# Attention groups A and B of a two-layer encoder: one unit per step, or two units with dense products between

## Chip, cores and metric

The kernel runs on one core of a Trainium2 chip. The metric is the device time of one execution in microseconds (us). Its engines are named as in the profile: PE multiplies matrices (PEld is its loading of weights), DVE, ACT and POOL work element by element, SP issues most transfers (DMAs).

## What is computed

Two layers of an encoder on 1024 tokens of width 1024, all in float32. In each layer one projection feeds three groups of heads: A is attention over three dilations, B is windowed attention with a sink, C is a matrix memory (mLSTM) in both directions. Their outputs are joined, projected and added; a gated feed-forward network and a gated embedding follow.

```python
for i in range(DEPTH):
    h = rmsnorm(x, attn_norm[i])
    z = h @ w_in[i]
    ...
    ya = dilated_attention(qa, ka, va, bias_a)
    yb, _ = banded_attention(qb, kb, vb, bias_b, WINDOW_B, WINDOW_B, 1, sink=sink_logits[i])
    yc = mlstm_mixer(qc, kc, vc, oc, gc, qk_conv[i], gate_bias[i], mlstm_norm[i])
    x = x + concatenate([ya, yb, yc]) @ w_out[i]
    ...
```

## The kernel before

Activations lie with features on the 128 partitions and tokens along the free axis. A **dense** product (`product`, L210 to L223) computes 128 features by 512 tokens: for each of 8 slices of the input three matmuls of 128x512 (L219 to L221: high by high, high by low, low by high part), 24 in all, into one of two PSUM banks kept for it (tag "d"). The high and low parts of a weight tile come from `split` (L130 to L134): a cast on ACT (L133, tile `wh`) and a subtraction (L134, `wl`).

`mixers` runs three generators side by side (L1137): `attend` (group A in `group_a`, then group C in `group_c`), `project` (all dense products of the input projection, and the convolution of C) and `side` (C's gates, and `combine_a`, which joins A's dilations). `mix` (L60 to L84) goes on with the stream whose sum of yielded costs is lowest; a yield is thus a place where other streams' instructions may come in between, and its number says how much of the others. A second `mix` (L1224) runs group B beside the output projection.

**Group A** has 24 units per layer: 3 pairs of heads, 2 sets of dilations, 4 pairs of token tiles. For each unit `score` multiplies queries by keys (L531, L533, L539, tile `psc`, operands of 64 rows), adds bias and takes the maximum on DVE (L551), and the exponential on ACT (L552) into two tiles `pr`. `flip` transposes the two `pr` on PE (L565, `ppt`, 8 transposes) and copies them to two tiles `pT` (DVE L570, ACT L568). `weigh` multiplies values by `pT` (L586, `po`, 64 columns wide) and copies the result to `u` (DVE L589 to L594). In a step i the kernel issues score(i), weigh(i-2), flip(i-1), and then yields.

**Group B** has 16 units: 8 token tiles T by 2; `score` (L709), `flip` (L731), and per T one `weigh` (L754) and one `turn` (transposes of the scale, L764). It yields after each unit.

**combine_a** makes per pair of heads a small table (`mj`, `pst`, `join`), spreads it to four tiles `f` (ACT, L659), transposes each (PE L664, `pf`) and multiplies `u` by it (DVE L666).

**Group C** follows: values of the keys by exponents (`pk`, `ke`, `pl`, a scan along the pieces in `sc`, `cst`), then 8 pieces, of each `decay` (a DMA into two tiles `ee`, an edge cut on POOL, 12 exponentials on ACT), `score` (`pss`, `psi`, L992, L997) and `weigh` (`pso`, L1010 to L1023). `ee` and `it` come from a pool of 7 buffers (`aslot`), three for each piece.

The tiles `pr`, `pT`, `f`, `th` and many others come from one pool of half tiles, and there are ten:

```python
def half(self, s, dt=F32):
    return self.sm.tile([P, 512], dt, tag="s2", name=self.nm(s), bufs=10)
```

In layer 0 the input is not normalised ahead of the projection: each dense result is multiplied by `self.r[hf]`, two half tiles (`rs`, from `rstd`) that live until the last dense product of the projection has been copied out (L401). In layer 1 `self.r` is None.

The program's order is not the order of the Python calls alone. A scheduler takes the recorded instructions and their pools, and sets for each engine one fixed list; an instruction whose buffer isn't free is put behind others that can go. Each engine then runs its list in order.

Of the kernel before, what the change touches and what calls it, by code (L numbers as in the profile page):

```python
# [34 lines left out]
NCH = S // P  # L35
# [47 lines left out]
class Trunk:  # L83
# [388 lines left out]
    def group_a(self, z):  # L472
# [4 lines left out]
        units = [(p, g, i) for p in range(3) for g in range(2) for i in range(NCH // 2)]  # L477
# [3 lines left out]
        def tables(p):  # L481
            n = 2 * NCH * P
            va = self.att.tile([P, n + 768], F32, tag="va", name=self.nm("va"), bufs=2)
            b0, b1 = self.aslot("b").rearrange("p (h w) -> p h w", h=2), va[:, n:]
            eng = nc.sync if p else nc.gpsimd

            nc.gpsimd.memset(b0[0:64, :, 256:384], NEG)
            nc.gpsimd.memset(b0[64:128, :, 384:512], NEG)
            self.toeplitz(b0[:, :, 0:256], 0, 2 * p, 2, 256, 191, P, eng)
            self.toeplitz(b0[0:64, :, 384:512], 0, 2 * p, 2, P, 191, 64, eng)  # L490
            self.toeplitz(b0[64:128, :, 256:384], 0, 2 * p, 2, P, 255, 64, eng)
            for i in range(3):
                self.toeplitz(b1.rearrange("p (h i w) -> p h i w", h=2, i=3)[:, :, i], 1, 2 * p, 2, P, i * PL1 + 127, P, eng)
            st["b", p], st["va", p] = (b0, b1), va

        def begin(p):
            if p == 0:
                tables(p)
            n, va = NCH * P, st.pop(("va", p))
            vs = [va[:, i * n : i * n + n].rearrange("p (t h d) -> p t h d", t=NCH, h=2) for i in range(2)]  # L500
            vt = z.pop(("v", p))
            self.values([vt[:, T * P : T * P + P] for T in range(NCH)], vs[0])
            self.values([vt[:, T::8] for T in range(NCH)], vs[1])
            del vt
            st["v", p] = vs

            z["s", p] = self.sm.tile([P, 2, 2, 2, NCH], F32, tag="stat", name=self.nm("stat"), bufs=2)
            z["o", p] = self.aslot("u"), self.aslot("u")

        def tiles(g, i):  # L510
            return (2 * i, 2 * i + 1) if g == 0 else (i, i + 4)
# [9 lines left out]
        def score(u):  # L521
            p, g, i = u
            (qn, qr), kr = z["q", p], z["k", p]
            pss = [self.bank("psc") for _ in range(2)]
            for s, T in enumerate(tiles(g, i)):
                ws, ts = slice(s * 256, s * 256 + 256), slice(T * P, T * P + P)
                for e, hp in enumerate(heads):
                    k = kr[hp].rearrange("p (r n) -> p r n", r=8)
                    o = pss[e][:, ws]
                    if g == 1:  # L530
                        nc.tensor.matmul(o, qr[hp, ts], k[:, T % 4 :: 4], start=True, stop=True)  # L531
                    elif T < NCH - 1:
                        nc.tensor.matmul(o, qn[hp, ts], k[:, :, 16 * T : 16 * T + 32], start=True, stop=True)  # L533
                if g == 0 and T == NCH - 1:
                    for m, n in ((0, 112), (16, 0)):
                        for e, hp in enumerate(heads):
                            k = kr[hp].rearrange("p (r n) -> p r n", r=8)
                            o = pss[e][:, ws].rearrange("p (r m) -> p r m", r=8)[:, :, m : m + 16]
                            nc.tensor.matmul(o, qn[hp, ts], k[:, :, n : n + 16], start=True, stop=True)  # L539
            prs = [self.half("pr") for _ in range(2)]  # L540
            for s, T in enumerate(tiles(g, i)):
                w = slice(s * 256, s * 256 + 256)
                for e in range(2):
                    nm, zs = (z["s", p][:, g, j, e, T : T + 1] for j in range(2))
                    o, sc, b = prs[e][:, w], pss[e][:, w], bias(p, g, T, e)
                    if g == 0:
                        sc = sc.rearrange("p (r m) -> p m r", r=8)
                        o, b = (x.rearrange("p (m r) -> p m r", r=8) for x in (o, b))
                    else:
                        o, sc = (x.rearrange("p (i w) -> p i w", i=2) for x in (o, sc))  # L550
                    nc.vector.tensor_tensor_reduce(o, sc, b, -1.0, 3e38, OP.add, OP.min, nm)  # L551
                    nc.scalar.activation(prs[e][:, w], prs[e][:, w], AF.Exp, bias=nm, scale=-1.0, accum_out=zs)  # L552
            st[u] = prs
            if g == 1 and i == 3:
                z.pop(("q", p)), z.pop(("k", p)), st.pop(("b", p))

        def flip(u):
            p, g, i = u
            pTs = []
            for e, pr in enumerate(st[u]):  # L560
                pt = self.bank("ppt")
                for b in range(4):

                    c = b if g == 0 else b % 2 * 2 + b // 2
                    nc.tensor.transpose(pt[:, c * P : c * P + P], pr[:, b * P : b * P + P], self.ident)  # L565
                pT = self.half("pT")
                if e:
                    nc.scalar.copy(pT, pt)  # L568
                else:
                    nc.vector.tensor_copy(pT, pt)  # L570
                pTs.append(pT)
            st[u] = pTs

        def weigh(u):
            p, g, i = u
            pTs = st.pop(u)
            v = st["v", p][g]
            po = self.bank("po")[:, 0:256]
            T = 2 * i
            if g == 0:  # L580
                steps = ((T + 1, 128, 384, 0), (T, 0, 128, 0), ((T + 2) % NCH, 384, 512, 128))
            else:
                steps = ((i, 0, 256, 0), (i + 4, 256, 512, 0))
            for n, (t, c0, c1, o0) in enumerate(steps):
                for e, hp in enumerate(heads):
                    nc.tensor.matmul(po[hp, o0 : o0 + c1 - c0], v[:, t, e, :], pTs[e][:, c0:c1], start=n == 0, stop=n == len(steps) - 1)  # L586
            us = z["o", p][g]
            if g:
                nc.vector.tensor_copy(us.rearrange("p (r n) -> p r n", r=8)[:, i::4], po.rearrange("p (i n) -> p i n", i=2))  # L589
            elif i < 3:  # L590
                nc.vector.tensor_copy(us[:, 64 + T * P : 320 + T * P], po)
            else:
                nc.vector.tensor_copy(us[:, 832:1024], po[:, 0:192])
                nc.vector.tensor_copy(us[:, 0:64], po[:, 192:256])  # L594
            if g == 1 and i == 3:
                st.pop(("v", p))
                z["u", p] = True

        n = len(units)
        for i in range(n + 2):  # L600
            cost = 0.0
            if i < n:
                p = units[i][0]
                if units[i][1:] == (0, 0):
                    while ("k", p) not in z:
                        yield None
                    begin(p)
                    cost += 2000.0
                score(units[i])
                cost += 1000.0  # L610
                if units[i][1:] == (0, 3) and p < 2:
                    tables(p + 1)
            if 0 <= i - 2:
                weigh(units[i - 2])
                cost += 1000.0
            if 0 <= i - 1 < n:
                flip(units[i - 1])
                cost += 1000.0
            yield cost

    def combine_a(self, z):

# [51 lines left out]
    def group_b(self, li, z, yT):  # L674

        nc = self.nc
        units = [(T, j) for T in range(NCH) for j in range(2)]
        heads = (slice(0, 64), slice(64, 128))
        st = {}

# [91 lines left out]
        while "qb1" not in z:  # L772
            yield None
        begin()
        n = len(units)
        for i in range(n + 5):
            cost = 0.0
            if i < n:
                score(units[i])
                cost += 900.0  # L780
            if i % 2 == 1 and 0 <= i - 3 < n:
                weigh((i - 3) // 2)
                cost += 1600.0
            if i % 2 == 0 and 0 <= i - 4 < n:
                turn((i - 4) // 2)
                cost += 300.0
            if 0 <= i - 1 < n:
                flip(units[i - 1])
                cost += 700.0
            if cost:  # L790
                yield cost

    def turn(self, li, yT):

# [912 lines left out]
```

## Time and profile before

| | us |
|---|---|
| median of three runs (lowest, highest) | 2758.97 (2756.2, 2760.41) |
| the profiled execution, its span | 2764.66, 2762.9 |
| PE busy over the span | 2653.5 |
| DVE, ACT, POOL busy | 1874.0, 1129.6, 690.2 |

How to read it: the profiled execution is 5.7 us longer than the median, and 1.8 us lie around its span. The chain of work that ended last lies on PE for 82% of the span. Layer 0's groups A and C with the input projection stand from 61.7 to 465 us of the span, layer 1's from 1500 to 1817 us; group B stands from 485 to 564 us and from 1837 to 1915 us. Rows of the trace name an instruction by engine, line and tiles (out<-in); `x8` means eight instructions in a row; a product of float32 operands shows as two.

### The profile page before, as it was taken

The page shows a single profiled execution, that of the slowest core. Times are in us where ns is not written, and L with a number is a line of the kernel's source. Part 1 is how long each engine was busy: PE and PEld are TensorE (multiplying, and loading weights), DVE is VectorE, ACT ScalarE, POOL GpSimd, SP SyncE. Part 2 cuts the span into 40 slices and gives each one's busy share as a digit, 9 for nine tenths or more (in the row PEclk, how much of TensorE's full clock was granted, in tenths as well). Part 3 has the DMA queues.
Part 4 walks back from the last instruction along what each step waited for, and adds up shares of the span by engine and source line. Part 5 has one row for each costly group of instructions (what it writes and reads, how often), then busy time and mean ns, then how long its engine had stood idle before and what let it go on. Part 6 is the DMA issues. An engine that isn't in the chain of part 4 may idle for free.

```text
span 2762.9 us, 37720 instructions
## 1 busy us (share of the span) xinstructions
PE 2653.5 (96%) x13906; PEld 2118.3 (77%) x13906; DVE 1874.0 (68%) x3119; ACT 1129.6 (41%) x2317; POOL 690.2 (25%) x544
## 2 busy tenths in 40 slices
PE   7999988998999999999999999989899999999997
PEld 5777766676888888888777778867678888888887
DVE  8645776569877775755655448664897777685646
ACT  5443243544333334234444433544443333242444
POOL 3112434136333330000121122431553333100002
PEclk9999998998999999999999999989999999999998
DMA  4010145131333338752321012442233333496424
GB/s 148 28 66 24 46 107 155 72 137 58 145 145 126 141 111 311 268 168 92 123 77 54 31 39 67 116 154 74 106 114 132 139 136 122 162 330 226 156 69 137
DMA packets 165340, 339.34 MB, mean 123 GB/s; under 512 B 18233, under 2 KB 57185, under 8 KB 165156
## 3 DMA queue, kind: packets, MB, share of 16 engines
q1 hardware_dynamic: 161460, 325.27, 34.7%
q0 software_dynamic: 3696, 11.66, 1.2%
q8 instruction: 110, 1.80, 0.3%
q14 instruction: 74, 0.61, 0.1%
HBM read 246.56 MB, written 90.30 MB: 122 GB/s over the span
## 4 chain that ended last, share of the span: by engine, by line
PE 82%; DVE 8%; issue 3%; DMA 2%; POOL 2%; ACT 2%; SPq 0%; DVEq 0%; POOLq 0%; ACTq 0%
PE pd L1270 9%; PE pd L1271 9%; PE pd L1269 9%; PE pd L219 9%; PE pd L220 9%; PE pd L221 9%; PE pd L1438 5%; PE pd L1437 5%; PE pd L1436 5%; PE po L586 1%; PE ppt L565 1%; DVE x L1234 1%; PE psc L709 1%; PE po L754 1%; PE psc L533 1%
## 5 line engine op out<-in xcount | busy, mean ns | idle before, releaser
L1270 PE MATMUL pd<-r,wf 128*128 128x512 f32 x1232 | 491.0, 399 | 24.0 <-POOL r L1229 13.2
L1269 PE MATMUL pd<-r,wf 128*128 128x512 f32 x1232 | 488.4, 397 | 10.0 <-ACT r L1228 10.0
L1271 PE MATMUL pd<-r,wf 128*128 128x512 f32 x1232 | 486.4, 395 | 0.0
L219 PE MATMUL pd<-h,wh 128*128 128x512 f32 x832 | 340.1, 409 | 13.0 <-ACT h L133 7.1
L220 PE MATMUL pd<-h,wh 128*128 128x512 f32 x832 | 329.9, 396 | 3.2 <-DVE h L134 1.7
L221 PE MATMUL pd<-h,wl 128*128 128x512 f32 x832 | 328.2, 395 | 1.0 <-DVE wl L134 1.0
L1270 PEld LDWEIGHTS pd<-r,wf 128*128 128x128 f32 x1232 | 233.8, 190 | 85.5 <-POOL r L1229 19.9
L1269 PEld LDWEIGHTS pd<-r,wf 128*128 128x128 f32 x1232 | 233.6, 190 | 66.0 <-ACT r L1228 12.6
L1271 PEld LDWEIGHTS pd<-r,wf 128*128 128x128 f32 x1232 | 234.3, 190 | 52.5
L1437 PE MATMUL pd<-f,f 128*128 128x512 f32 x616 | 239.9, 389 | 1.1 <-DVE f L134 1.1
L1438 PE MATMUL pd<-f,f 128*128 128x512 f32 x616 | 239.7, 389 | 0.0
L1436 PE MATMUL pd<-f,f 128*128 128x512 f32 x616 | 236.3, 389 | 0.1
L1288 DVE TENSOR_TENSOR g<-g,pd 128x512 f32<-128x512 f32 x264 | 175.7, 680 | 60.7 <-PE pd L1271 59.1
L134 DVE TENSOR_TENSOR wf<-s,wf 128x512 fp32r<-128x512 f32 x176 | 161.9, 921 | 64.1 <-ACT wf L133 63.0
L133 ACT CAST wf<-s 128x512 fp32r<-128x512 f32 x176 | 106.5, 617 | 222.3 <-POOL s L200 63.9
L219 PEld LDWEIGHTS pd<-h,wh 128*128 128x128 f32 x832 | 158.2, 190 | 48.5 <-ACT h L133 7.1
L347 POOL TENSOR_TENSOR acc<-acc,sq 128x512 f32<-128x512 f32 (+1 forms) x22 | 29.6, 1344 | 654.5 <-ACT sq L346 654.2
L220 PEld LDWEIGHTS pd<-h,wh 128*128 128x128 f32 x832 | 158.5, 190 | 35.5 <-DVE h L134 2.6
L221 PEld LDWEIGHTS pd<-h,wl 128*128 128x128 f32 x832 | 158.2, 190 | 35.7 <-DVE wl L134 1.9
L134 POOL TENSOR_TENSOR wl<-wr,wh 128x1024 fp32r<-128x1024 f32 (+1 forms) x44 | 109.3, 2483 | 251.2 <-ACT wh L133 142.1
L134 DVE TENSOR_TENSOR f<-wr,f 128x512 fp32r<-128x512 f32 x132 | 90.1, 688 | 90.4 <-ACT f L133 86.3
L133 ACT CAST wh<-wr 128x1024 fp32r<-128x1024 f32 (+1 forms) x112 | 113.7, 1016 | 70.8 <-PE pd L220 49.4
(310 smaller groups left out, 5279.6 us busy)
## 6 DMA issues: line engine op xcount, KB each, us to landing
wr<-w_up SPq DMA_DIRECT2D x88, 512.0 KB, 4.3
bs<-wf SPq DMA_DIRECT2D x88, 512.0 KB, 2.7
f<-bs SPq DMA_DIRECT2D x176, 256.0 KB, 3.5
wr<-w_in SPq DMA_DIRECT2D x52, 512.0 KB, 3.6
wr<-w_down SPq DMA_DIRECT2D x88, 256.0 KB, 5.3
wr<-ple_gate SPq DMA_DIRECT2D x40, 512.0 KB, 3.5
bd<-g SPq DMA_DIRECT2D x66, 256.0 KB, 2.0
b<-bd SPq DMA_DIRECT2D x66, 256.0 KB, 5.6
```

The costliest lines, as they stand in the source:

```text
L133: self.pin(nc.scalar.copy(hi[:, cs], src))
L134: self.pin((eng or nc.vector).tensor_tensor(lo[:, cs], src, hi.bitcast(F32)[:, cs], OP.subtract))
L219: nc.tensor.matmul(ps, hi[:, ks], rh, start=k == 0, stop=False)
L220: nc.tensor.matmul(ps, hi[:, ks], rl, start=False, stop=False)
L221: nc.tensor.matmul(ps, lo[:, ks], rh, start=False, stop=k == n - 1)
L1269: nc.tensor.matmul(ps, hi[:, ks], rh, start=k == 0, stop=False)
L1270: nc.tensor.matmul(ps, hi[:, ks], rl, start=False, stop=False)
L1271: nc.tensor.matmul(ps, lo[:, ks], rh, start=False, stop=k == KT // 2 - 1)
L1288: add = lambda out, a, b, op=OP.add: nc.vector.tensor_tensor(out, a, b, op)
L1436: nc.tensor.matmul(ps, lh[:, cs], rh, start=k == 0, stop=False)
L1437: nc.tensor.matmul(ps, lh[:, cs], rl, start=False, stop=False)
L1438: nc.tensor.matmul(ps, ll[:, cs], rh, start=False, stop=k == NPAIR - 1)
```

## The change

Group A now takes units by twos. A step issues both scores, yields (so dense products of `project` come in), then issues the weighing of the preceding two units and the transposes of these two, and yields again. The yields sum to what they were. Group B does the same with the two units of a token tile; `turn` comes after the transposes, and the first step now yields 3300 with no `weigh` in it.

```diff
--- before.py
+++ after.py
@@ -596,27 +596,30 @@
                 st.pop(("v", p))
                 z["u", p] = True
 
-        n = len(units)
-        for i in range(n + 2):
-            cost = 0.0
-            if i < n:
-                p = units[i][0]
-                if units[i][1:] == (0, 0):
-                    while ("k", p) not in z:
-                        yield None
-                    begin(p)
-                    cost += 2000.0
-                score(units[i])
-                cost += 1000.0
-                if units[i][1:] == (0, 3) and p < 2:
-                    tables(p + 1)
-            if 0 <= i - 2:
-                weigh(units[i - 2])
-                cost += 1000.0
-            if 0 <= i - 1 < n:
-                flip(units[i - 1])
-                cost += 1000.0
-            yield cost
+
+        pairs = list(zip(units[::2], units[1::2]))
+        last = ()
+        for pair in pairs:
+            p = pair[0][0]
+            if pair[0][1:] == (0, 0):
+                while ("k", p) not in z:
+                    yield None
+                begin(p)
+                yield 2000.0
+            for u in pair:
+                score(u)
+            if pair[1][1:] == (0, 3) and p < 2:
+                tables(p + 1)
+            yield 2000.0
+            for u in last:
+                weigh(u)
+            for u in pair:
+                flip(u)
+            last = pair
+            yield 4000.0
+        for u in last:
+            weigh(u)
+        yield 2000.0
 
     def combine_a(self, z):
 
@@ -674,7 +677,6 @@
     def group_b(self, li, z, yT):
 
         nc = self.nc
-        units = [(T, j) for T in range(NCH) for j in range(2)]
         heads = (slice(0, 64), slice(64, 128))
         st = {}
 
@@ -772,23 +774,19 @@
         while "qb1" not in z:
             yield None
         begin()
-        n = len(units)
-        for i in range(n + 5):
-            cost = 0.0
-            if i < n:
-                score(units[i])
-                cost += 900.0
-            if i % 2 == 1 and 0 <= i - 3 < n:
-                weigh((i - 3) // 2)
-                cost += 1600.0
-            if i % 2 == 0 and 0 <= i - 4 < n:
-                turn((i - 4) // 2)
-                cost += 300.0
-            if 0 <= i - 1 < n:
-                flip(units[i - 1])
-                cost += 700.0
-            if cost:
-                yield cost
+        for T in range(NCH + 1):
+            if T < NCH:
+                for j in range(2):
+                    score((T, j))
+                yield 1800.0
+            if T:
+                weigh(T - 1)
+            if T < NCH:
+                for j in range(2):
+                    flip((T, j))
+            if T:
+                turn(T - 1)
+            yield 3300.0
 
     def turn(self, li, yT):
```

What the scheduler makes of it is shown at three places; lines in the changed file are two or three lower than before behind the edits.

**PE, group A of layer 1** (`psc` scores, `po` weighing, `ppt` transposes, `pd` dense). Before, one unit:

```order
L221 MATMUL pd_13612<-h_11814,wl_13258 128x512
L531 MATMUL psc_13664<-z_13130,z_12892 128x256
L531 MATMUL psc_13665<-z_13130,z_12892 128x256
L531 MATMUL psc_13664<-z_13130,z_12892 128x256
L531 MATMUL psc_13665<-z_13130,z_12892 128x256
L586 MATMUL po_13680<-pT_13643,va_12844 64x256
L586 MATMUL po_13680<-pT_13650,va_12844 64x256
L586 MATMUL po_13680<-pT_13643,va_12844 64x256
L586 MATMUL po_13680<-pT_13650,va_12844 64x256
L565 MATMUL ppt_13686<-ident,pr_13622 128x128 x4
L565 MATMUL ppt_13693<-ident,pr_13623 128x128 x4
L219 MATMUL pd_13612<-h_11820,wh_13257 128x512
```

Now, from the end of a pair's scores to the weighing of the preceding pair:

```order
L531 MATMUL psc_13647<-z_13144,z_12906 128x256
L219 MATMUL pd_13626<-h_11796,wh_13235 128x512
L220 MATMUL pd_13626<-h_11797,wh_13235 128x512
L221 MATMUL pd_13626<-h_11796,wl_13236 128x512
L219 MATMUL pd_13626<-h_11802,wh_13235 128x512
L220 MATMUL pd_13626<-h_11803,wh_13235 128x512
L221 MATMUL pd_13626<-h_11802,wl_13236 128x512
L586 MATMUL po_13668<-pT_13578,va_12814 64x256
L586 MATMUL po_13668<-pT_13585,va_12814 64x256
L586 MATMUL po_13668<-pT_13578,va_12814 64x256
L586 MATMUL po_13668<-pT_13585,va_12814 64x256
L586 MATMUL po_13674<-pT_13592,va_12814 64x256
```

Scores, weighing and transposes stood next to each other; now a run of dense products stands between scores and weighing, and each run is twice as long.

**ACT, layer 0, the joining of A's second pair of heads** (`f` the third of its four tiles, `wh` weight casts of the projection). Before:

```order
L552 ACTIVATE pr_2078,stat_1789<-pr_2078,stat_1789 128x256 x2
L568 COPY pT_2107<-ppt_2102 128x512
L659 COPY f_2113<-join_1925 128x512
L552 ACTIVATE pr_2136,stat_1789<-pr_2136,stat_1789 128x256 x2
L552 ACTIVATE pr_2137,stat_1789<-pr_2137,stat_1789 128x256 x2
L568 COPY pT_2167<-ppt_2162 128x512
L659 COPY f_2169<-join_1925 128x512
L133 CAST wh_2322<-wr_2055 128x1024
```

Now:

```order
L1110 ACTIVATE sg_3214<-sg_3214 128x512 x2
L133 CAST wh_3621<-wr_3413 128x1024
L133 CAST wh_3766<-wr_3619 128x1024
L133 CAST wh_3936<-wr_3764 128x768
L662 COPY f_2118<-join_1936 128x512
L568 COPY pT_2161<-ppt_2156 128x512
L568 COPY pT_2175<-ppt_2170 128x512
L662 COPY f_2180<-join_1936 128x512
L552 ACTIVATE pr_2212,stat_1803<-pr_2212,stat_1803 128x256 x2
```

The third `f` stood right behind its pair's exponentials, ahead of most weight casts. It now stands behind the projection's last weight cast (`wh_3936`), with A's last copies and exponentials behind it.

**PE, layer 0, from the end of group A to group C** (`pst`, `pf` the joining, `pvt` transposes of values, `pk`, `pl` group C). Before, in A's joining:

```order
L220 MATMUL pd_2387<-h_230,wh_2057 128x512
L221 MATMUL pd_2387<-h_229,wl_2058 128x512
L664 MATMUL pf_2396<-ident,f_2391 128x128 x4
L219 MATMUL pd_2387<-h_235,wh_2057 128x512
L220 MATMUL pd_2387<-h_236,wh_2057 128x512
L221 MATMUL pd_2387<-h_235,wl_2058 128x512
L219 MATMUL pd_2387<-h_241,wh_2057 128x512
L220 MATMUL pd_2387<-h_242,wh_2057 128x512
L221 MATMUL pd_2387<-h_241,wl_2058 128x512
L219 MATMUL pd_2387<-h_247,wh_2057 128x512
```

Now:

```order
L586 MATMUL po_2307<-pT_2282,va_1389 64x256
L640 MATMUL pst_2315<-mj_2313,div_111 64x32 x16
L447 MATMUL pvt_2332<-ident,z_2074 128x128 x4
L447 MATMUL pvt_2338<-ident,z_2074 128x128 x4
L667 MATMUL pf_2385<-ident,f_2380 128x128 x4
L667 MATMUL pf_2407<-ident,f_2399 128x128 x4
L667 MATMUL pf_2425<-ident,f_2417 128x128 x4
L667 MATMUL pf_2440<-ident,f_2434 128x128 x4
L447 MATMUL pvt_2446<-ident,z_2344 128x128 x4
L447 MATMUL pvt_2452<-ident,z_2344 128x128 x4
L921 MATMUL pk_2915<-ident,cv_2521 128x128 x4
L921 MATMUL pk_2924<-ident,cv_2521 128x128 x4
L935 MATMUL pl_2945<-vc_1806,ke_2920 64x65 x8
```

Before, dense products stood between all of these, and in group C too (15 to 21 between its runs). Now 717 dense matmuls stand in one run behind the scores of A's pair (third pair of heads, first set, tiles 4 to 7); the next row is the transposes of the late `f`, and from there to group C's last product no dense matmul is left. In layer 1 they still alternate.

## Rows read from the trace of the kernel before

**Rows 1.** Timeline of PE, 78.0 to 82.2 us: start, length, instructions.
```profile
78.26 0.39 PE L221 MATMUL pd<-h,wl 128*128 128x512 f32 x1
78.58 1.13 PE L531 MATMUL psc<-z,z 64*128 64x256 f32 x8
79.64 1.09 PE L586 MATMUL po<-pT,va 128*64 128x256 f32 x12
80.66 1.09 PE L565 MATMUL ppt<-ident,pr 128*128 128x128 f32 x8
81.51 0.48 PE L219 MATMUL pd<-h,wh 128*128 128x512 f32 x1
81.83 0.39 PE L220 MATMUL pd<-h,wh 128*128 128x512 f32 x1
82.06 0.40 PE L221 MATMUL pd<-h,wl 128*128 128x512 f32 x1
```

**Rows 2.** Timeline from 61.7 us: two units' scores in one run, the first exponential.
```profile
61.72 2.00 PE L533 MATMUL psc<-z,z 64*128 64x256 f32 x16
...
63.35 0.51 ACT L552 ACTIVATE pr<-pr,stat 128x256 f32<-128x256 f32 x1 [0.32 <-DVE stat L551]
```

**Rows 3.** PE's waits, 60 to 330 us: total us, times, longest.
```profile
PE pd L219 <- DVE z L401: 2.9, 1, 2.9
```

**Rows 4.** PE's waits, 330 to 365 us.
```profile
PE pl L937 <- DVE ke L926: 10.0, 2, 9.7
```

**Rows 5.** Three stretches: us, busy of PE, PEld, DVE, ACT, POOL, granted clock.
```profile
330.00:365.00 35.00, 24.85 (x182) 18.98 (x180) 29.49 (x27) 9.65 (x16) 11.18 (x7) 0.85 0.31 83
381.49:458.88 77.39, 77.39 (x737) 62.58 (x736) 48.69 (x113) 36.81 (x107) 31.01 (x33) 1.00 0.39 104
468.00:472.00 4.00, 0.00 (x0) 0.00 (x0) 1.30 (x5) 2.38 (x4) 1.41 (x2) 0.50 0.53 167
```

**Rows 6.** Groups of PE by line, 381.5 to 458.9 us: count, busy, mean ns.
```profile
L219 PE MATMUL pd<-h,wh 128*128 128x512 f32 x77 | 31.7, 411 | 0.0
```

**Rows 7.** Timeline of the joining of group A, 207 to 217 us.
```profile
208.06 0.41 DVE L631 TENSOR_TENSOR mj<-stat,mod 128x256 f32<-128x256 f32 x1
...
213.50 0.19 DVE L652 TENSOR_TENSOR join<-join 128x32 f32<-128x32 f32 x1
```

**Rows 8.** Groups by line, 60 to 480 us: count, busy us, mean ns.
```profile
L552 ACT ACTIVATE pr<-pr,stat 128x256 f32<-128x256 f32 x96 | 47.6, 497 | 48.2 <-DVE stat L551 48.2
...
L926 DVE TENSOR_TENSOR ke<-pk,cols 128x512 f32<-128x512 f32 x12 | 7.6, 680 | 1.4 <-PE pk L923 1.4
...
L946 DVE TENSOR_TENSOR_SCAN sc<-sc,sc 128x455 f32<-128x455 f32 x6 | 7.8, 1312 | 6.0 <-ACT sc L944 6.0
...
L832 DVE SCALAR_TENSOR_TENSOR cv<-th,cv 128x512 f32<-128x512 f32 x12 | 7.8, 688 | 3.6 <-ACT th L831 3.6
...
L937 PE MATMUL pl<-vc,ke 128*64 128x65 f32 x168 | 7.7, 242 | 10.0 <-DVE ke L926 10.0
```

**Rows 9.** Timeline, 451 to 470 us: group C's last two pieces.
```profile
451.59 1.95 DVE L992 SCALAR_TENSOR_TENSOR ee<-pss,ee 128x384 f32<-128x384 f32 x4 [0.22 <-PE pss L982]
...
453.45 1.15 DVE L997 SCALAR_TENSOR_TENSOR it<-psi,cols 128x195 f32<-128x195 f32 x4
...
454.51 0.86 POOL L967 TENSOR_SCALAR_AFFINE_SELECT ee<-ee 128x768 f32<-128x768 f32 x1 [1.98 <-DMA ee<-md]
...
455.41 1.87 ACT L970 ACTIVATE ee<-ee,cols 128x128 f32<-128x128 f32 x6 [0.97 <-POOL ee L967]
...
456.43 1.62 PE L1009 MATMUL pso<-vc,ee 128*64 128x65 f32 x48
...
465.21 1.03 DVE L1010 TENSOR_TENSOR it<-it,pso 128x390 f32<-128x390 f32 x2
...
466.96 0.96 DVE L1017 TENSOR_TENSOR it<-it,den 128x768 f32<-128x768 f32 x1
```

**Rows 10.** DMA issues: count, KB each, median us to landing.
```profile
ee<-md SPq DMA_DIRECT2D x32, 384.0 KB, 7.5
```

## Prediction

> **What bounds the kernel now.** I read the chain of waits first: it lies on PE for 82% of the span. So a change gains where PE's list gets shorter, and loses where PE stands still. The timeline of PE in group A then shows how one unit is packed: scores, weighing and transposes without a pause, dense products on both sides [rows 1]. PE's waits come next: between 60 and 330 us the only one over 1 us is a dense product that stands 2.9 us for a result to be copied out [rows 3]; the large one, 10.0 us, is group C's `pl` behind `ke` [rows 4]. Last come the windows: over 77.39 us, in which seven of C's eight pieces run, PE is busy all the time, at full clock, while DVE works 48.69 us of it [rows 5]. That cover is made by dense products: 77 of L219 [rows 6], so with L220 and L221 some 232. The reader should keep this in mind: C's long chains over DMA, POOL, ACT and DVE cost PE nothing because dense products stand between them.
>
> **What the change removes.** From the last dense matmul ahead of a unit to the second behind it is 81.83 - 78.26 = 3.57 us; less two dense steps of 0.23 (82.06 - 81.83), the unit takes 3.11 [rows 1]. What it holds is less. Two units' scores in one run take 2.00, one unit's 1.13 [rows 1, 2], so scores are worth 0.87; eight transposes 0.85 (80.66 to 81.51); I take the weighing at 0.85 too (its 1.02 has a boundary in it) [rows 1]. That is 2.57, and 0.54 are left for three boundaries between kinds of products, about 0.18 each; from transposes to dense there is nearly nothing. Before, two units have six such boundaries; now four (dense to scores, scores to dense, dense to weighing, weighing to transposes). A pair thus saves about 0.34. Of the 24 pairs in both layers I count 21 (three of layer 0 stand in the stretch below, which is priced whole): 7.1 us. Group B loses about one boundary per token tile: 16 x 0.17 = 2.7. Together **-9.8 us**; bounds 0 (a boundary costs the same wherever it is put) and 16 (three saved for each pair). The Trainium skill has the same rule (TensorEngine Tiling (Array Packing), Key Properties): a change of tiling mode drains TensorE, which speaks for operands of 64 rows or columns standing together. By that rule alone the change gains; it is the first rival.
>
> **What it moves.** The half tiles are ten. Now four `pr` and four `pT` live at once between a pair's scores and its weighing, where one unit per step needs less; in layer 0 the two `rs` are held until the last dense product is copied out. That is ten, and the third `f` of the second joining finds none. The order shows what follows: on ACT this `f` stands behind the last weight cast, and on PE 717 dense matmuls stand in one run (about 165 us by 0.23 each, no longer than they were), with the end of A, its joinings, and all of C behind them, bare. In layer 1 there is no `rs`, and dense products still alternate. SP's list keeps C's loads in the same sequence, and they can land no earlier than C's buffers come free.
>
> The bare stretch, from the last dense product to the last result of C's last piece:
> - End of A. PE's own work: scores 2.0 for two units, weighing of six 5.1, transposes of four 3.4, 40 transposes for `f` and values 4.3 (0.85 for eight), `pst` about 1, boundaries 1: 17 us. To it come the joining of the last pair, 208.06 to 213.69 or 5.6 us on DVE and PE in turn [rows 7], and the last pair's chain from scores to exponentials to copies, about 2: **25**, bounds 20 (the transposes of values cover the joining) and 30.
> - The convolution's last products on DVE, 12 of 688 ns [rows 8]: **8**. They stand ahead of `ke` in DVE's queue.
> - C's own values: `ke` 7.6, then the scan 7.8, one behind the other on DVE, and `pl` 7.7 on PE, partly beside them [rows 8]: 15.4 to 23, taken **20**.
> - Eight pieces. DVE's part of one is 1.95 + 1.15 + 2.71 (465.21 to 467.92) = 5.8 [rows 9]. The ring of seven buffers is longer: with three for a piece, two pieces need a DMA of 7.5 [rows 10], the cut 0.86, exponentials 1.87, half of L992 1.0, `pso` 1.62 [rows 9], in all 12.9, with issues about 14.5, so 7.25 for one. The last piece, which has no cover today either, takes 458.88 to 467.92, 9.0. Bounds 5.8 and 9.0; I take the ring: **58**.
>
> Sum 25 + 8 + 20 + 58 = **111 us**; ends 20 + 8 + 15 + 46 = 89 and 30 + 8 + 23 + 72 = 133.
>
> What the same work costs PE before: 17 for A's end; 10 for C's values (`pl` 7.7 [rows 8] and 24 transposes, 2.6); seven pieces, 77.39 less 232 x 0.23 = 24 [rows 5, 6]; the last piece 9; and the wait of 10 [rows 4], which falls away since `ke` is waited for within the bare stretch. In all 70. In the long run of dense products a copy-out may once stand behind the convolution on DVE; rows 3 give 2.9 for such a stall, I take 1.5 (0 to 2.9).
>
> **111 - 70 + 1.5 - 9.8 = +33 us.** The profiled execution, 2764.7 (span 2762.9 and 1.8 around it), becomes 2798; the median shown is 5.7 lower, so **2792**. A rule that speaks against this change stands in the Trainium skill (Perfetto Trace Analysis, Optimization Strategy): stretches bound by different engines may run better interleaved. It gives no size. The rows above agree with it: DVE's 48.69 us lie wholly under a busy PE.
>
> **Rivals.**
> 1. Faster: 2750. The boundaries gain their 9.8, and the bare stretch takes no more than PE spends on this work today, because DVE, ACT and POOL have run ahead under the 717 dense matmuls. The point that decides: below 78 us (70 + 9.8 - 1.5) the change gains; at 72 or less it does so measurably. For it: a list isn't a time, and DVE is free for 28.7 of 77.39 us [rows 5]. Against: nothing of C's values stands ahead of the run's end in DVE's list, and eight pieces at DVE's 5.8 are 46, which with 20 for A's end and 15 for C's values make 81. The tiling rule above speaks for this rival.
> 2. Half clock over C. The granted clock was 0.50, the 1.2 GHz level, where PE stood idle at 468 to 472, and 0.85 on average over 330 to 365 us with its wait of 10 [rows 4, 5]. Bare, PE works about half of the time. If from C's values on it is at the lower level, `pl` and the transposes take 10 us more, half of them on the chain (25), and `pso` 1.6 more for two pieces (8.1 each, 64): 25 + 8 + 25 + 64 = 122, +44, so 2803. By the Trainium skill (TensorE: Matmul & The Clock Gate, What's actually happening) the lower level is the default and activity lifts it.
> 3. Pairs wait for exponentials. Eight for a pair at 497 ns [rows 8], from 1.6 us behind the first score (61.72 to 63.35 [rows 2]), end at 5.6. PE comes to the last transposes after 2.0 for scores, six to nine dense steps (1.4 to 2.1), 2.0 for weighing and 1.3 for twelve transposes: 6.7 at the earliest. That leaves 1.1, about what one weight cast or two copies in ACT's queue take. If every second pair lost 1.1, and the rest held, the saving would be gone: +43, 2802.
> 4. No measurable change: bare for 73 to 83 us, all low ends together.
>
> **How the numbers follow.** Forecast as such 0.56, half clock 0.2, late exponentials 0.1, no change 0.07, faster 0.07. About 0.2%, 5.5 us, is what a measurement of this kernel can tell from none. Faster 0.07, same 0.07, slower 0.86. Low end: 89 us bare gives 2759 + 89 - 70 + 1.5 - 9.8 = 2770. High end: 133 gives 2814; I go to 2816, for the lower clock over more than C's part. This leaves the first and the fourth rival outside, and a little above.
>
> **What would show it.** In layer 0, PE in one run of dense products, then some 111 us in which PE is busy about half of the time, its waits now on `ee` (from DMA and DVE), on `ke` and on the joining, the clock at 0.50 in parts; the last piece ends some 38 us later than 467.92 less what A's first nine pairs saved. The four parts 25, 8, 20 and 58 can each be read there. In layer 1, group A without new waits and about 4 us shorter; each layer's group B shorter by 1 to 2. The prediction is wrong if layer 0's dense run is broken up, if C's pieces come at under 5.8 us, if layer 1's pairs wait for exponentials, or if boundaries don't cost what the unit's 3.11 us say.

## The result and the profile after

The changed kernel takes **2795.2 us** (median of four runs, 2794.17 to 2798.51) where before takes 2759.14: a ratio of 1.0129, interval 1.0116 to 1.0142, or 36 us slower. Forecast were 2792 and +33. The run profiled lasted 2794.17 us, its span 2792.4 (before 2764.66 and 2762.9); these two lie only 29.5 us apart, since the profiled run of before was itself 5.7 us above its median.

The end of the long dense run and of C's last piece, from the timeline of the changed kernel (start, length, engine, instructions):

```profile
386.49 0.39 PE L221 MATMUL pd<-h,wl 128*128 128x512 f32 x1
...
387.64 0.62 ACT L662 COPY f<-join 128x512 f32<-128x512 f32 x1 [10.72 <-DVE z L401]
388.31 0.66 PE L667 MATMUL pf<-ident,f 128*128 128x128 f32 x4 [1.43 <-ACT f L662]
...
501.28 0.18 DVE L1011 SCALAR_TENSOR_TENSOR den<-it 128x12 f32<-128x12 f32 x1
...
501.97 0.96 DVE L1015 TENSOR_TENSOR it<-it,den 128x768 f32<-128x768 f32 x1
```

The third `f` is copied as soon as the last dense result has been multiplied by `rs` (DVE `z`, L401), after ACT had waited 10.72 us for it. (The scores ahead of the run, at 222.14 us, are of L531 and so of the second set of the third pair of heads, not of the first set as said above; the count of ten half tiles is the same.) From 386.72 (386.49 and a step of 0.23) to 502.93 no dense product runs: a bare stretch of **116 us**, bare because no dense product covers its waits, where 111 were worked out. Its three parts in windows of the changed kernel (us; busy PE, PEld, DVE, ACT, POOL; granted clock):

```profile
386.90:412.20 25.30, 19.49 (x176) 16.11 (x176) 16.69 (x46) 15.57 (x44) 7.58 (x8) 0.93 0.30 69
412.20:436.80 24.60, 11.98 (x164) 9.81 (x164) 21.70 (x30) 13.19 (x23) 3.77 (x4) 0.72 0.12 39
436.80:502.90 66.10, 45.33 (x608) 38.93 (x604) 48.83 (x122) 32.57 (x97) 21.54 (x26) 0.77 0.44 118
```

A's end took 25 (forecast 25), convolution and C's values 25 (28), the eight pieces 66 (58). The 25 in the middle is 10 for the convolution (forecast 8) and 14 for C's values (20), by this row of the timeline:

```profile
412.73 10.21 DVE L830 SCALAR_TENSOR_TENSOR cv<-th,cv 128x512 f32<-128x512 f32 x12
```

DVE's work, which before lay under a PE busy for all of 77.39 us [rows 5], is now waited for; in the 66.10 us of the pieces DVE is busy for 48.83. PE's waits of the changed kernel, 386 to 503 us (total, times, longest):

```profile
PE pso L1007 <- DVE ee L990: 17.0, 12, 2.9
PE pl L935 <- DVE ke L924: 8.8, 5, 5.4
PE pf L667 <- ACT f L662: 5.7, 3, 3.0
PE pk L921 <- DVE cv L830: 3.9, 2, 2.4
```

Before had 10.0 us for `ke` [rows 4] and little else here. In layer 1 (whose group A begins with scores at 1425 us in before, not at 1500) the dense products still alternate, but group A has waits that it hadn't. The changed kernel, 1455 to 1700 us:

```profile
PE ppt L565 <- DVE stat L551: 2.6, 1, 2.6
PE ppt L565 <- ACT pr L552: 2.2, 5, 0.5
PE pf L667 <- ACT f L662: 1.0, 1, 1.0
```

### The profile page after: what moved, and what is told of

It reads as the page before. It is cut to its first block, busy times and chain, and to the rows that moved or that the text cites. A ratio compares the mean times of both kernels' runs of the same rounds, so it can differ in the third digit from the quotient of the medians.

```text
span 2792.4 us, 37810 instructions
## 1 busy us (share of the span) xinstructions
PE 2653.8 (95%) x13906; PEld 2137.2 (77%) x13906; DVE 1879.7 (67%) x3119; ACT 1135.8 (41%) x2317; POOL 689.7 (25%) x544
## 4 chain that ended last, share of the span: by engine, by line
PE 82%; DVE 9%; issue 3%; ACT 2%; DMA 2%; POOL 1%; SPq 0%; DVEq 0%; POOLq 0%; ACTq 0%
PE pd L219 10%; PE pd L1268 10%; PE pd L220 9%; PE pd L221 9%; PE pd L1269 9%; PE pd L1267 9%; PE pd L1435 5%; PE pd L1436 5%; PE pd L1434 5%; PE ppt L565 1%; PE po L586 1%; DVE x L1232 1%; DMA ee<-md 1%; PE ppt L733 1%; PE psc L711 1%
## 5 line engine op out<-in xcount | busy, mean ns | idle before, releaser
L347 POOL TENSOR_TENSOR acc<-acc,sq 128x512 f32<-128x512 f32 (+1 forms) x22 | 29.5, 1343 | 653.4 <-ACT sq L346 653.1
```

## Experiments

Times are set against runs of the kernel before on the same chip: 2762.3 us for half11, yr_late, b_only and sw_adjacent, 2761.7 for the other four, which ran later on another chip. Ratios are compared across the two; the difference of two ratios is good to some 4 to 5 us either way.

**One half tile more (half11).**

```diff
-        return self.sm.tile([P, 512], dt, tag="s2", name=self.nm(s), bufs=10)
+        return self.sm.tile([P, 512], dt, tag="s2", name=self.nm(s), bufs=11)
...
-                st["m", T] = self.sm.tile([P, 2, 2, 2], F32, tag="mb", name=self.nm("mb"), bufs=4)
+                st["m", T] = self.sm.tile([P, 2, 2, 2], F32, tag="mb", name=self.nm("mb"), bufs=2)
```

> The changed kernel with eleven half tiles instead of ten (and two buffers instead of four for B's small `mb` tiles, to make room); nothing else differs, and the dense products of layer 0 stand between A's pairs, the joinings and C's pieces again. Theory 1 (the cost is the missing half tile alone, which strips A's end and C of cover): the bare stretch of 116 us is gone and the time falls below before. By boundaries alone 2759 - 9.8 = 2749; if layer 0 behaves as layer 1 does in the trace of the changed kernel (its A gains only about 0.6 us net, since its pairs wait some 5 us for maxima and exponentials; each B gains 1.6): 2759 - 1.2 - 3.2 = 2755. Theory 2 (pairs themselves are slow, since they wait for their exponentials): at least 2785, no better than 10 us below the changed kernel.

Measured: 2755.2, ratio 0.9972 (0.9962 to 0.9982), 7.0 us faster than before; set against 2759 that is 2752, between theory 1's two sums. Two rows of its timeline mark the same work, from the dense product behind the scores of the same pair (224.07 in the changed kernel) to the end of C:

```profile
225.50 0.51 PE L219 MATMUL pd<-h,wh 128*128 128x512 f32 x1
...
464.07 0.96 DVE L1015 TENSOR_TENSOR it<-it,den 128x768 f32<-128x768 f32 x1
```

Here 239.5 us, in the changed kernel 502.93 - 224.07 = 278.9. Both contain the 717 dense products, so the missing half tile costs **39 us**. As those take 162.65 in the changed kernel (224.07 to 386.72), the rest costs 77 under cover and 116 without it. Theory 1 holds. (The times alone make it 43: 1.0129 against 0.9972, good to some 5 us.) The window of half11 shows what the 39 are made of:

```profile
225.50:465.03 239.53, 223.04 (x1663) 179.85 (x1661) 158.71 (x261) 90.25 (x211) 83.67 (x69) 0.97 0.29 76
```

Here PE stands still for 16.5 us; in the three windows of the bare stretch above for 39.2, or 23 more. The other 16 are the same products taking longer (76.8 busy, here 223.04 - 162.65 = 60.4) at granted clocks of 0.72 to 0.93, where this window has 0.97; how many of these 16 lie on the chain isn't shown. The pairs of half11 still wait in layer 0, 60 to 300 us:

```profile
PE ppt L565 <- DVE stat L551: 2.6, 1, 2.6
PE ppt L565 <- ACT pr L552: 2.4, 4, 1.0
PE pf L667 <- ACT f L662: 1.0, 1, 1.0
```

**The same shortage in layer 1 (hold_layer1).** Two half tiles are held there through the projection; a multiplication ahead of each return is added, whose result nobody reads.

```diff
+            hold = []
+            if not self.r:
+                hold = [self.half("hold") for _ in range(2)]
+                for t in hold:
+                    nc.vector.memset(t, 1.0)
...
+            for t in hold:
+                nc.vector.tensor_tensor(t, t, z["qb1"][:, 512:1024], OP.mult)
+            del hold
```

> The changed kernel, ten half tiles, but in layer 1 too two half tiles are taken at the start of the projection and given back after its last dense product (they are set to one, and at the end multiplied by a finished tile; nothing reads them). Layer 1 had no such tiles, and its dense products alternate with A and C. Theory 1 (two long-lived half tiles beside a pair's four `pr` and four `pT` make the bare stretch): layer 1 gets a run of 717 dense products and a bare stretch of about 116 us as well, which costs what layer 0's did: 500.33 less 462.43, the last `pso` of layer 0 in the changed kernel and in half11, and 1.4 for their different starts, 39 us. Some 75 us above before, 2834 where before is 2759. Theory 2 (layer 0's stretch comes from the multiplication by `rs`, which layer 1 hasn't): no more than 5 us above the changed kernel, 2795 to 2800.

Measured: 2850.5, ratio 1.0319 (1.0303 to 1.0335), 89 us above before. Layer 1 now has its own dense run and bare stretch, 1791.67 to 1910.34, or 119 us, in the timeline of hold_layer1:

```profile
1791.44 0.39 PE L221 MATMUL pd<-h,wl 128*128 128x512 f32 x1
1794.88 0.66 PE L667 MATMUL pf<-ident,f 128*128 128x128 f32 x4 [3.05 <-ACT f L662]
...
1909.38 0.96 DVE L1015 TENSOR_TENSOR it<-it,den 128x768 f32<-128x768 f32 x1
```

That settles the cause, as theory 1 has it. The size, some 52 us for layer 1 by the times (1.0319 less 1.0129 of 2760; some 5 us either way), is 13 above what I wrote. The traces show it directly: windows from the dense product behind the scores of the pair that precedes the run to the end of C, in layer 1 of the changed kernel and of hold_layer1.

```profile
1625.00:1850.87 225.87, 218.84 (x1663) 177.64 (x1661) 143.15 (x243) 96.82 (x223) 70.78 (x57) 1.00 0.31 80
1629.03:1910.34 281.31, 238.91 (x1663) 198.26 (x1661) 145.33 (x245) 97.56 (x223) 73.07 (x57) 0.91 0.24 64
```

That is 55 us. Less some 162.6 for the 717 dense products, the rest costs 63 under cover in layer 1, where it was 77 in layer 0, and 119 bare, where it was 116. Most of what differs I had left out: in layer 0 the bare stretch swallows a 10 us wait that layer 1 doesn't have. Two rows of half11's timeline, the first `pl` of layer 0 and of layer 1:

```profile
351.12 1.14 PE L935 MATMUL pl<-vc,ke 128*64 128x65 f32 x16 [9.65 <-DVE ke L924]
...
1704.04 0.69 PE L935 MATMUL pl<-vc,ke 128*64 128x65 f32 x16 [1.33 <-DVE ke L924]
```

The wait is 8.3 us shorter in layer 1, and the 16 `pl` behind it take 0.69 us there and not 1.14 (the granted clock of layer 1's window is 1.00, of layer 0's 0.97). With the longer bare stretch (119 against 116) the shorter wait makes up 11 of the 16 us between 39 and 55.

**Loads of `yr` behind those of `ee` (yr_late).**

```diff
-                nc.sync.dma_start(y[:, :384], self.yd[(4 * i + j) * P : (4 * i + j) * P + P])
+                self.tc.keep_in_program_order(nc.sync.dma_start(y[:, :384], self.yd[(4 * i + j) * P : (4 * i + j) * P + P]))
```

> The changed kernel with the loads of `yr` kept in the program's order, so that SP issues all loads of `ee` ahead of them; PE's list is the same up to C's last product. C's eight pieces took 66 us in the changed kernel and not 58. Theory 1 (the ring was longer than priced, because SP's next `ee` stood behind a load of `yr` that waited for a piece's finished output): the pieces take 56 to 60 us, and the time is about 2787, or up to 3 us more since `yr` now lands after C. Theory 2 (the lower clock made them 66): the pieces take 64 to 67 us, and the time is 2795 to 2798.

Measured: 2792.4, ratio 1.0109 (1.0096 to 1.0123). Set against 2759 that is 2789, within theory 1's range; but the interval overlaps that of the changed kernel, so the time alone doesn't decide. SP's waits of the changed kernel, 436 to 505 us, name what was removed, loads that wait for a finished piece to be stored (`yd<-yc`):

```profile
SPq L798 <- DMA yd<-yc: 30.4, 5, 9.3
```

Windows of the changed kernel, C's first piece (first `pss` to its `den`) and the seven periods behind it, each from one `den` to the next:

```profile
436.83:444.98 8.15, 6.61 (x121) 5.63 (x120) 6.69 (x14) 6.74 (x17) 0.00 (x0) 1.00 0.03 8
444.98:501.28 56.30, 38.70 (x492) 33.30 (x488) 40.59 (x105) 25.80 (x81) 21.54 (x26) 0.74 0.51 137
```

The same windows of yr_late:

```profile
438.85:449.83 10.98, 10.34 (x108) 8.71 (x108) 6.53 (x13) 6.88 (x17) 0.00 (x0) 0.50 0.03 8
449.83:500.60 50.77, 35.50 (x502) 29.98 (x500) 40.42 (x106) 25.57 (x79) 20.10 (x26) 0.84 0.57 162
```

Both theories have a part. Seven periods take 50.8 instead of 56.3, on average 7.25 each instead of 8.0. Nearly all of these 5.5 us lie in one period, from the fourth `den` to the fifth; the changed kernel, then yr_late:

```profile
467.80:479.63 11.83, 9.06 (x90) 7.91 (x87) 6.24 (x17) 5.41 (x17) 4.00 (x5) 0.66 0.49 142
471.71:478.69 6.98, 5.91 (x90) 4.88 (x87) 6.01 (x17) 2.75 (x10) 2.82 (x4) 0.99 0.50 148
```

The other six take 44.5 and 43.8. Layer 0 of hold_layer1 runs the list of the changed kernel once more, and its seven periods take as long as there:

```profile
448.61:504.94 56.33, 38.94 (x492) 33.50 (x488) 41.17 (x105) 25.93 (x81) 20.92 (x26) 0.71 0.53 137
```

So the 56.3 are no chance of one execution, and the queue did lengthen the ring. But in the long period PE is also at its lower clock for most of the time (0.66, in yr_late 0.99) and is busy for 9.06 us with products that take 5.91 in yr_late, so not all 5.5 us need be the queue's own. And the first piece took 2.8 us longer at a granted clock of 0.50, 1.2 GHz, than at 1.00; all pieces together took 63.4, not 56 to 60.

**Group B alone (b_only).** Group A as before, ten half tiles; B as in the change (the lines taken out are those of the change).

```diff
+        for T in range(NCH + 1):
+            if T < NCH:
+                for j in range(2):
+                    score((T, j))
+                yield 1800.0
...
+            yield 3300.0
```

> The kernel before with the change in group B alone; A goes by single units. Theory 1 (B saves about one boundary per token tile, 0.17 us x 16 = 2.7; its stretch was 1.6 us shorter in each layer of the changed kernel): 2756, each layer's B 1.3 to 1.6 us shorter and all else as before. Theory 2 (boundaries cost nothing; B's gain came from what stood around it): 2759, within 1 us. The spread of the runs of before (2756.2 to 2760.4) is as large as the difference, so the stretch of B in the trace decides rather than the time.

Measured: 2759.05, ratio 0.9989 (0.9980 to 0.9998), 3.2 us faster, near the edge of what can be told. The stretch of B decides: windows from the first to the last dense product of the output projection, layer 0 in before and b_only, then layer 1 in before_11 (the next run, whose B is that of before; in before itself layer 1 has a lower granted clock, 0.98, and takes 130.6) and b_only.

```profile
480.51:611.07 130.56, 130.41 (x656) 95.64 (x654) 77.69 (x176) 60.47 (x155) 27.85 (x37) 0.98 0.32 116
480.61:609.58 128.97, 128.72 (x655) 96.32 (x654) 78.39 (x176) 62.64 (x155) 28.64 (x37) 0.98 0.33 115
1831.12:1960.49 129.37, 129.11 (x655) 94.58 (x654) 77.68 (x176) 60.37 (x155) 27.87 (x37) 0.99 0.34 117
1831.62:1959.25 127.63, 127.38 (x655) 95.26 (x654) 77.99 (x176) 62.61 (x155) 28.62 (x37) 0.99 0.33 116
```

B is 1.6 and 1.7 us shorter at equal clocks: theory 1. A's steps thus bear the whole loss: 1.0129 against 0.9989 is 39 us, good to some 4.

**The eleventh tile without pairs (before_11).** The two lines of half11, in the kernel before.

```diff
-        return self.sm.tile([P, 512], dt, tag="s2", name=self.nm(s), bufs=10)
+        return self.sm.tile([P, 512], dt, tag="s2", name=self.nm(s), bufs=11)
...
```

> The kernel before with eleven half tiles and two `mb`, as half11 has them; PE's list is the same as before. Theory 1 (a single unit per step never runs out of ten): no change, within 0.1%. Theory 2 (half11 is faster for its eleventh tile, not for its pairs): 3 us or more below before.

Measured: 2759.9, ratio 0.9991 (0.9982 to 1.0000). Theory 2's 3 us aren't excluded by the interval, which reaches to 5.0 below before; the 39 us are. The trace speaks for theory 1: from a matmul of layer 0's normalisation to its first `pl` this kernel takes 301.1 us (52.41 to 353.47) and before 301.5, where half11 takes 299.1.

**More dense products ahead of weighing and transposes (flip_later).** half11, with

```diff
-            yield 2000.0
+            yield 3600.0
             for u in last:
                 weigh(u)
...
-            yield 4000.0
+            yield 2400.0
```

> half11 with the dense products of a pair dealt out otherwise: 3600 behind the scores and 2400 behind the transposes, not 2000 and 4000 (12 to 15 dense matmuls stand between scores and weighing, not 6 to 9). The boundaries are as many as in half11; only the exponentials get 1.4 us more. Theory 1 (half11 lost its boundaries' gain to transposes that waited for maxima and exponentials, 2.6 + 2.4 us in layer 0, 2.6 + 2.0 in layer 1): these 9.6 us shrink to 2 or less and the time falls by about 8, to 15 below before. Theory 2 (the waits only move, to the first pair or to copies): 7 to 9 below before, as half11. Where sw_adjacent, 16.3 below before, got its gain is told by this too: what flip_later does not reach, up to 7 us, is the price of the boundary saved there.

Measured: 2749.2, ratio 0.9956 (0.9943 to 0.9968), 12.6 us faster than before and 5.6 more than half11. The waits of transposes fell from 9.6 to 3.9. flip_later, 60 to 300 us:

```profile
PE ppt L565 <- DVE stat L551: 1.2, 1, 1.2
PE ppt L565 <- ACT pr L552: 1.1, 2, 0.5
```

flip_later, 1400 to 1700 us:

```profile
PE ppt L565 <- ACT pr L552: 1.0, 2, 0.5
PE psc L531 <- DVE u L591: 0.8, 1, 0.8
...
PE ppt L565 <- DVE stat L551: 0.6, 1, 0.6
```

The gain is as large as these waits that went, but part of them moved, as theory 2 has it: transposes of the joining wait 3.5 us for `f`, not 1.9 as in half11, and scores 0.8 for `u`. The time lies between the theories, and its interval (9 to 16 us below before) reaches both; theory 1 in kind, not in size.

**Weighing next to the scores (sw_adjacent).** half11; A and B (yields of B 3400 and 1700):

```diff
             for u in pair:
                 score(u)
+            for u in last:
+                weigh(u)
             if pair[1][1:] == (0, 3) and p < 2:
                 tables(p + 1)
-            yield 2000.0
-            for u in last:
-                weigh(u)
+            yield 3000.0
             for u in pair:
                 flip(u)
             last = pair
-            yield 4000.0
+            yield 3000.0
```

> Eleven half tiles as in half11; in A and B a step's weighing of the preceding pair stands directly behind the scores, then dense products, then the transposes alone, then dense products. Boundaries per pair that cost about 0.17: dense to scores, scores to weighing, weighing to dense, three instead of four (transposes have the dense products' form on both sides); and the exponentials have the weighing and a longer dense run before their transposes. Theory 1 (boundaries and the waits for exponentials are what is left to gain): 40 pairs x 0.17 = 7 less than half11, and the pairs' waits for maxima and exponentials, some 5 us in each layer, mostly gone: 2739 to 2744. Theory 2 (only the waits matter, a boundary has no price of its own): 2745 to 2750. Theory 3 (neither): as half11.

Measured: 2745.9, ratio 0.9940 (0.9928 to 0.9953): 16.3 below before and 9.3 below half11, where theory 1 asked for 11 to 16. Set against its own before it is 2743 where before is 2759, within theory 1's range, but the interval reaches into theory 2's, since some waits stayed. Whether a boundary has a price of its own is read where next to no wait is in the way, in group B (0.2 us of PE's waits in flip_later, none here): windows as for b_only, layer 1 of flip_later, whose B is that of half11, and of sw_adjacent.

```profile
1823.37:1950.38 127.01, 126.72 (x656) 94.77 (x654) 78.59 (x176) 62.60 (x155) 28.67 (x37) 1.00 0.34 119
1818.09:1943.36 125.27, 125.27 (x656) 95.32 (x655) 77.68 (x176) 61.92 (x155) 26.86 (x37) 1.00 0.34 121
```

Both have the same products at full clock and eight token tiles with one boundary less each: 1.7 us, or 0.2 for one. Theory 1 holds in kind.

**The same with a longer dense run ahead of the transposes (sw_longer).**

```diff
-            yield 3000.0
+            yield 3900.0 if last else 5700.0
             for u in pair:
                 flip(u)
+            yield 2100.0 if last else 300.0
             last = pair
-            yield 3000.0
```

> sw_adjacent with more dense products between group A's weighing and its transposes (yields 3900 and 2100, not 3000 and 3000; 5700 and 300 in the first step, which has no weighing). In sw_adjacent the transposes still waited for maxima and exponentials for 2.9 us in layer 0 and 3.2 in layer 1. Theory 1 (these are all that is left of the pairs' waits): 4 to 6 us less than sw_adjacent, some 21 below before. Theory 2 (the waits come back as waits on copies, since transposes and the next scores lie closer): within 2 us of sw_adjacent.

Measured: **2739.2**, ratio 0.9919 (0.9907 to 0.9932), 22.5 us faster than before: the best version here, faster than both kernels, and some 6 below sw_adjacent (0.9940 less 0.9919): theory 1. The transposes' own waits gave only 3 of it (6.1 to 3.1 us in both layers). sw_longer, 1400 to 1700 us:

```profile
PE ppt L565 <- ACT pr L552: 1.0, 2, 0.5
PE pf L667 <- ACT f L662: 0.9, 1, 0.9
PE psc L531 <- DVE pT L570: 0.6, 1, 0.6
PE ppt L565 <- DVE stat L551: 0.2, 1, 0.2
```

Against flip_later, whose dense run ahead of A's transposes is about as long, it gains 10 us more. Waits in A explain under 3; the rest goes with one boundary less for a pair, 7 us (good to some 5) for 40 pairs or about 0.17 each, which agrees with the 0.2 read in B.

## Why the prediction was right

- **The mechanism** was right: the third `f`, the run of 717, the bare stretch. half11 takes it away, hold_layer1 makes it a second time.
- **"Sum 25 + 8 + 20 + 58 = 111"** came out at 116. A's end was right; the convolution was 2 too low, C's values 6 too high (two of their six scans, at 438.44 and 439.91 us, run beside the first piece), the pieces 8 too low. That the sum missed by no more than 5 is partly luck. The ring of seven buffers, with its 1.6 us for issues that no row stood behind, gave "7.25 for one" and left out that SP's next `ee` stands behind a load of `yr` that waits for a finished piece. I had read SP's list only for the order of the `ee` loads among themselves. Without that wait the periods are 7.25 us on average, but that they agree to the digit is chance: their granted clock was 0.84, how much is owed to it stays open, and no run with more buffers shows that the ring is the limit.
- **"In all 70"**, what the same work costs under cover, is 77 in half11. Two parts of the 7 can be read in the traces: the first of the late `pf` waits 1.0 us for `f`, and PE is at the lower clock for some us behind the 10 us wait (16 `pl` in 1.14 us, not 0.69), which the term didn't hold. The errors of 5 and 7 nearly cancel: 39 measured, 41 by the sum. Less the 7.0 that half11 gained, the 39 make 32, the low end of what was measured (32 to 39).
- **"1.5" for a stall in the dense run**: PE has no such wait in the changed kernel, and the 2.9 us of before [rows 3] are gone there.
- **"Together -9.8"**: half11 is 7.0 below before. The boundaries gave what was put down, and waits that weren't took part of it back. Windows from a matmul of the layer's normalisation to its first `pl`, with the same products in them, layers 0 and 1 of before, then of half11:

```profile
52.36:353.82 301.46, 287.03 (x1697) 222.71 (x1695) 188.32 (x385) 121.49 (x311) 78.92 (x61) 0.99 0.15 48
1393.45:1708.51 315.06, 310.34 (x1802) 242.07 (x1800) 180.54 (x382) 133.77 (x335) 67.46 (x49) 0.99 0.13 42
52.06:351.12 299.06, 282.41 (x1696) 223.65 (x1695) 187.27 (x385) 122.82 (x311) 78.76 (x61) 0.98 0.16 48
1389.49:1704.04 314.55, 306.59 (x1802) 243.37 (x1801) 184.10 (x382) 135.09 (x335) 67.68 (x49) 0.99 0.14 42
```

  PE's busy time fell by 4.6 and 3.8 us, 0.35 for each of the 24 pairs, where 0.34 was worked out. But its idle time rose by 2.2 and 3.2 us, although two stalls went (the 2.9 of [rows 3], and 2.2 for a copy of ACT in layer 1): the transposes' waits of about 5 us in each layer are new. So A gained 2.4 and 0.5 us where 7.1 were put down. B gained 1.6 and 1.7 (b_only) where 2.7 stood for both. (The upper bound of 16 doesn't follow from three boundaries for each of the 21 pairs and one per token tile, which make 13; nothing rests on it.)
- **Rivals.** The third, late exponentials, was there in small: the transposes wait 9.6 us in half11, about what that rival asked for. Half of it is a single wait of 2.6 in each layer, and that one is for a maximum on DVE, which the rival didn't work out: the pair's scores, begun at 94.53 us, find DVE in the scans of C's gates. half11, layer 0:

```profile
97.63 2.25 DVE L859 TENSOR_TENSOR_SCAN gm<-fg,ig 32x1024 f32<-32x1024 f32 x1
...
101.13 0.41 DVE L551 CUSTOM_DVE_ANT_1 pr<-psc,va 128x256 f32<-128x256 f32 x1
...
102.60 0.44 PE L565 MATMUL ppt<-ident,pr 128*128 128x128 f32 x2 [2.59 <-DVE stat L551]
```

  The forecast stood all the same, since the boundaries' gain, B's part and the stalls that went made up for these waits. The second rival, the lower clock, was there too (0.72 and 0.77), and the sum held nothing for it. One piece shows a price of 2.8 us, and the products of the bare stretch take 16 us longer than in half11, but what the clock cost on the chain wasn't measured: no run kept PE busy in it. The first and the fourth fell.
- In layer 1 the change was to shorten group A by 4 us and bring no new waits; neither came true. That its pairs wait for exponentials was named as a sign that the prediction is wrong, and for this part it was: the price of a boundary held, the claim that nothing else would wait did not. It is a small part of the +33.

## What to carry to other kernels

Count the buffers that are live between two yields before making a step larger: a tile that waits for the last of a long stream pushes everything behind it to the stream's end, and the cover of a whole stage goes with it; a tile that lives long in the same pool is what tips it. Where a list of instructions is fixed ahead, compare the two lists first: a run of 717 like instructions says more than any busy share. And place products that change the form of PE's operands next to each other, with the longest dense run ahead of what waits for DVE and ACT.

## What was not expected of the hardware

The same first piece of C, with the same products of PE in the same order, took 8.15 us at a granted clock of 1.00 and 10.98 at 0.50; in both kernels PE had been busy for about half of the time before it (11.98 of 24.60 us in the changed kernel, 12.40 in yr_late). So the clock at which the piece happens to begin is worth 2.8 us. And a load that waits in SP's queue for another engine's finished piece to be stored holds up the loads behind it: SP stood up to 9.3 us at a time here, and with those loads put last, seven periods took 50.8 us and not 56.3.
